# The modulation's matrix-vector product, moved from VectorE and GpSimd to quarters of the TensorE array

## The chip, the cores and the metric

The kernel runs on one core of a Trainium2 chip. A core has TensorE (PE, products), VectorE (DVE), ScalarE (ACT), GpSimd (POOL) and SyncE (SP, which here only issues transfers). The metric is the device time of one execution in microseconds (us). Before the change it is 2470.45 us, the median of three runs (2469.16 to 2474.44).

## The reference

Two blocks of a network for 512 tokens of width 2048, all in float32. The change touches the start of the first block, where a vector `c` of length 2048 gives each channel a shift, a scale and a gate:

```
c_act = silu(c)
mod = c_act @ w_ada + b_ada              # 2048 -> 3 * 2048
shift, scale, gate = split(mod, 3)
h = rms_norm(x) * (1 + scale) + shift
proj = h @ w_in                          # 2048 -> 5184
... recurrent branch, attention branch, their outputs y
x = x + gate * (y @ w_out)
```

The product `c_act @ w_ada` is one row times a matrix of 50 MB: little arithmetic per weight. Its first two thirds (shift and scale) are needed before any product with `w_in`, the last third (gate) only after both branches. A second block and a gated embedding follow.

## The kernel before

The tokens are kept transposed: a tile is 128 channels on the partitions by 512 tokens, and x is 16 such tiles, `xT[0]` to `xT[15]`. A product in float32 precision is made of three products in the faster type fp32r: each operand is split into a high part (a rounded copy, ScalarE) and a low part (the rest, VectorE), names `whi`, `wlo`, `hh`, `hl`, and `mm3` issues three TensorE products. These are the "split products" below. A product on unsplit float32 operands is used in few places: the sums over partitions with a tile of ones (`pnx`, `pada`) and `pR`, which spreads the norm over the partitions.

The program is written out in full, and a planner fixes its order: a "spine" of units (a block of weights, its split, its products) is walked in order, and side work written as generators is put between the products when the estimated clocks of class `Clock` say that what it waits for is there. Each engine then runs its own queue strictly in that order. SP's queue holds the loads; a load waits there until the buffer that it reuses is free, and everything behind it waits too. There are 78 buffers of 2 KB per partition for most tiles and 10 of 4 KB for weights.

The start of the spine is the embedding product (`pple`, 96 split products), meanwhile the squares of x are summed. Then come the products with `w_in`: `pearly` (four output tiles that are summed up in PSUM, two channel tiles at a time), `pp` (the others, in parts), later `ppan`. Those with channel tiles 2g and 2g+1 need group g of the modulation.

The modulation comes in eight groups `ada_group(g)`. A group is 16 pieces `wada` of 128 x 512 weights: piece k holds the rows of `w_ada` that meet `ccol[:, k]`, and its columns are the shifts and scales of 256 channels. VectorE multiplies most pieces by their `ccol` and adds them to one sum (`stt`, line 302); for the others ScalarE multiplies (line 314) and GpSimd adds them to a second sum (line 287). GpSimd joins the two, `ada_sum` adds over the partitions with four products with ones (`pada`), then `modT` gets the bias and `modulate` applies it to two tiles of x and splits them into `hh` and `hl`. Group 0 keeps its two sums apart. The gate (`ada_gate`) does the same with 64 pieces `wgate` in four groups, every second piece by ScalarE and GpSimd, while the recurrent branch (`prg`, `pig`, `xcl`) runs.

Of the kernel before, what the change touches and what calls it, by code (L numbers as in the profile page):

```python
# [11 lines left out]
AF = mybir.ActivationFunctionType  # L12
OP = mybir.AluOpType
# [8 lines left out]
NSLOT, NW = 78, 10                   # buffers of 2 KB and of 4 KB in each partition  # L22
LD, LS = 4, 3                        # units of weights loaded ahead, and split ahead
GSPLIT = (2, 3, 4, 5)                # first units, of which GpSimd takes the low parts
ADALD0, ADALD = 16, 4                # pieces of the modulation's weights loaded ahead, for the first group and later
POOL0, POOL = (1, 3, 4, 6, 8, 10), (1, 4, 7, 10, 13)  # pieces that ScalarE and GpSimd take
XF = 8                               # tiles of x loaded before the rest of the embedding's weights
XK = (2, 5, 6, 8, 10, 12, 14, 15)    # tiles of x squared before each of the first blocks of that product is copied
RB = 12                              # block of that product at which the norm of x starts
PLEG = 4                             # group of the modulation from which the product is stored  # L30
ORDER = (0, 1, 2, 10, 3, 11, 4, 12, 5, 13, 6, 14, 7, 15)  # columns of the first projection: 0-7 gate, 8-15 recurrence
GATEN = 4                            # position in that order at which the modulation's gate starts
FILL = (2, 3, 3, 3, 5)               # tiles of the first output between the pairs of heads
UPB, UPM = 3, 26                     # lead of the up projection of b; tile of the merge gates at which its loads start
WIDTH, STEPS = 2, 2                  # recurrences in flight; steps of one generator at a time
BACKLOG, LATE = 3.0, 5.0             # how far the other engines' work may run ahead of TensorE's (us, estimated)
# [3 lines left out]
def consts():  # L40
    """Constants that depend on shapes alone."""
# [43 lines left out]
def blocks():  # L85
    """The blocks (rows of tiles from, to, (columns from, to), ..) in which the weights are read."""
# [60 lines left out]
class Clock:  # L147
    """Rough times of the engines, by which the work is interleaved; nothing depends on it but the order."""
# [32 lines left out]
class Sides:  # L181
    """Work that is interleaved with the stream of projections: each generator yields the tiles that it waits for."""
# [54 lines left out]
class Unit:  # L237
    def __init__(self, src, shape, mm, pre=None, hold=1, half=False):
        """hold: the units whose weights are done with after this one; half: weights in the small slots."""
        self.src, self.shape, self.mm, self.pre, self.hold, self.half = src, shape, mm, pre, hold, half  # L240
        self.raw = self.hi = self.lo = None


def emit(ctx, tc, I, out):
# [122 lines left out]
    # ---------------------------------------------------------------- constants and loads  # L367
# [25 lines left out]
    # silu of c  # L393
# [13 lines left out]
    # ---------------------------------------------------------------- per-layer embedding product  # L407
# [36 lines left out]
    # ---------------------------------------------------------------- x, its norm, and the modulation  # L444
# [10 lines left out]
    def row_rsqrt(ssum, name, keep_cols=None, flag=None):  # L455
        """1 / rms of each token, on all partitions, from the sums of squares that each partition holds."""
# [25 lines left out]
    def x_stats():  # L482
# [15 lines left out]
        tt(xT[0], xT[0], R_["x"], OP.mult)  # L498
        gtt(xT[1], xT[1], R_["x"], OP.mult)
# [13 lines left out]
    def ada_sum(accs, js):  # L513
        ps = bank("pada")
        for j, jj in enumerate(js):
            for i, a in enumerate(accs):
                mm(ps[:, j:j + 1], a[:, jj * 128:(jj + 1) * 128], ones[:, 0:1], i == 0, i == len(accs) - 1)
        return ps

    def ada_group(g):  # L520
        accs = [slot([128, 512], "aacc") for _ in range(2)]
        a3 = [a.rearrange("p (s n) -> p s n", s=2) for a in accs]
        for k in range(16):
            w = ada_raw.pop((g, k))
            j = k in (POOL if g else POOL0)
            if g and k in (6, 9):
                x = xT[2 * g + k // 9]
                gtt(x, x, R_["x"], OP.mult)
            yield EAGER, [w]
            if k == 0:  # L530
                ts(a3[0], w, ccol[:, 0:1], None, OP.mult)
            elif k == 1:
                act(a3[1], w, AF.Identity, scale=ccol[:, 1:2])
            elif j:
                act(w, w, AF.Identity, scale=ccol[:, k:k + 1])
                gtt(a3[1], a3[1], w, OP.add)
            else:
                stt(a3[0], w, ccol[:, k:k + 1], a3[0], OP.mult, OP.add)
            ada_dma(g * 16 + k + 1 + (ADALD0 if g == 0 else ADALD))
            if g >= PLEG and stores:  # L540
                dma("G", *stores.pop(0))
        yield accs if g else accs[1:]
        r0 = WHERE["b_ada"]
        k0 = 2 * g
        if g == 0:
            ps = ada_sum(accs[1:], range(4))
            pre = small("apre")
            tt(pre[:, 0:2], ps[:, 0:2], cols[:, r0:r0 + 2], OP.add)
            stt(pre[:, 2:4], ps[:, 2:4], 1.0, cols[:, r0 + 16:r0 + 18], OP.add, OP.add)
            while issued["split"] < 6:  # L550
                split_next()
            yield accs[:1]
            ps = [ada_sum(accs[:1], (i, 2 + i)) for i in range(2)]
            while "scaled" not in ada:
                ada["stuck"] = True
                yield
            for i in range(2):
                tt(modT[:, i:i + 1], ps[i][:, 0:1], pre[:, i:i + 1], OP.add)
                tt(modT[:, 16 + i:17 + i], ps[i][:, 1:2], pre[:, 2 + i:3 + i], OP.add)
                modulate(i)  # L560
            dma("Q", cst[:, 128:], I["cst"][:, 128:])
            return
        gtt(accs[0], accs[0], accs[1], OP.add)
        yield accs[:1]
        ps = ada_sum(accs[:1], range(4))
        tt(modT[:, k0:k0 + 2], ps[:, 0:2], cols[:, r0 + k0:r0 + k0 + 2], OP.add)
        stt(modT[:, 16 + k0:18 + k0], ps[:, 2:4], 1.0, cols[:, r0 + 16 + k0:r0 + 18 + k0], OP.add, OP.add)
        for k in (k0, k0 + 1):
            modulate(k)

# [23 lines left out]
    def ada_gate():  # L594
# [11 lines left out]
        load(4)  # L606
        yield

        def sums(c, a):
            ps = ada_sum([a], range(4))  # L610
# [3 lines left out]
        due = None  # L614
        for c in range(4):
# [1587 lines left out]
```

## Time and profile before

| | |
|---|---|
| median of three runs | 2470.45 us |
| the profiled execution, its span | 2470.8 us |
| PE busy | 2389.4 us, 97% |
| VectorE, ScalarE, GpSimd busy | 62%, 39%, 16% |
| mean granted TensorE clock | 0.983 |

The profile is one execution on the chip. The span is cut in 40 slices on its page; digits are tenths of busy time, and `PEclk` the granted clock. All that the change touches lies in the first seven slices, of 62 us each:

```
PE   6898988999999999999999999999999999999998
DVE  7777899558786537747887725777424345333336
PEclk8998989999999999999999999999999999999999
```

A true float32 product shows as two records, each with its own load of weights; a split product as one. Matmuls are pipelined, so the time from one start to the next is what a product costs, not its shown length.

### The profile page before, as it was taken

What the parts mean: (1) busy time and instruction counts of PE and PEld (TensorE: products, weight loads), DVE (VectorE), ACT (ScalarE), POOL (GpSimd) and SP (SyncE); (2) the same over time, 40 slices, a digit from 0 to 9 for tenths busy, and PEclk for the clock granted to TensorE, in tenths of its full rate; (3) what the DMA queues carried; (4) which work ended last, traced back from release to release, by engine and by line L of the source; (5) the groups of instructions that cost most, each with busy time, mean ns of one, the idle gap of its engine ahead of it and who ended that gap; (6) DMA issues with size and microseconds to landing.
All of it is one profiled execution on the core that took longest, in us unless ns stands there. A gap on an engine that the chain in (4) does not pass through costs nothing.

```text
span 2470.8 us, 31047 instructions
## 1 busy us (share of the span) xinstructions
PE 2389.4 (97%) x11491; PEld 2007.0 (81%) x11491; DVE 1524.6 (62%) x2771; ACT 975.8 (39%) x1792; POOL 406.6 (16%) x479
## 2 busy tenths in 40 slices
PE   6898988999999999999999999999999999999998
PEld 5676766988888998888888888888888888888887
DVE  7777899558786537747887725777424345333336
ACT  5533555445443334334444414444323222222223
POOL 3454345023221200100000000000001200111201
PEclk8998989999999999999999999999999999999999
DMA  8775554233235533422222222222335633444633
GB/s 301 249 259 194 186 185 150 86 119 122 101 107 179 165 103 102 129 90 90 95 86 90 90 94 94 93 88 86 113 123 182 229 112 107 134 138 141 221 99 123
DMA packets 114760, 336.98 MB, mean 136 GB/s; under 512 B 15326, under 2 KB 15620, under 8 KB 114608
## 3 DMA queue, kind: packets, MB, share of 16 engines
q1 hardware_dynamic: 89712, 256.63, 31.7%
q0 software_dynamic: 24032, 77.22, 9.2%
q8 instruction: 90, 1.47, 0.2%
q10 hardware_dynamic: 864, 1.14, 0.1%
q14 instruction: 62, 0.51, 0.1%
HBM read 297.18 MB, written 37.75 MB: 136 GB/s over the span
## 4 chain that ended last, share of the span: by engine, by line
PE 71%; issue 10%; DVE 3%; DMA 1%; POOL 1%; ACT 0%; POOLq 0%; SPq 0%; DVEq 0%; ACTq 0%
PE pch L320 43%; PE ppan L320 11%; PE po L320 6%; PE psc L320 3%; PE pO L320 3%; PE pPT L324 2%; DVE wlo L283 1%; DVE agacc L302 0%; DVE cA L283 0%; DMA sguw<-in_sgu_w_dram 0%; PE pcs L320 0%; PE px L324 0%; DMA w1r<-in_cmp_w_k_dram 0%; PE pqT L324 0%; PE pcT L324 0%
## 5 line engine op out<-in xcount | busy, mean ns | idle before, releaser
L283 DVE TENSOR_TENSOR wlo<-wraw,whi 128x1024 fp32r<-128x1024 f32 (+5 forms) x399 | 479.3, 1203 | 219.3 <-ACT whi L314 214.0
L314 ACT ACTIVATE whi<-wraw 128x1024 fp32r<-128x1024 f32 (+5 forms) x403 | 399.8, 1002 | 287.5 <-PE pch L320 107.8
L320 PE MATMUL pch<-h2h,whi 128*128 128x512 f32 x1216 | 483.5, 398 | 0.0
L320 PE MATMUL pch<-h2h,wlo 128*128 128x512 f32 x1216 | 474.5, 390 | 0.0
L320 PE MATMUL pch<-h2l,whi 128*128 128x512 f32 x1216 | 474.4, 390 | 0.0
L320 PEld LDWEIGHTS pch<-h2h,wlo 128*128 128x128 f32 x1216 | 228.3, 188 | 49.2
L320 PEld LDWEIGHTS pch<-h2h,whi 128*128 128x128 f32 x1216 | 228.7, 188 | 41.2
L320 PEld LDWEIGHTS pch<-h2l,whi 128*128 128x128 f32 x1216 | 229.0, 188 | 40.5
L314 ACT ACTIVATE P<-psc,sm 128x512 f32<-128x512 f32 (+3 forms) x160 | 83.8, 527 | 137.1 <-DVE sm L306 101.8
L320 PE MATMUL pp<-hh,wlo 128*128 128x512 f32 x320 | 129.1, 403 | 6.8 <-DVE wlo L283 6.8
L320 PE MATMUL pp<-hh,whi 128*128 128x512 f32 x320 | 130.2, 407 | 2.2 <-DVE acc L283 2.2
L320 PE MATMUL pp<-hl,whi 128*128 128x512 f32 x320 | 129.1, 404 | 0.0
L320 PE MATMUL ppan<-whi,x2h 128*128 128x512 f32 (+1 forms) x320 | 111.0, 347 | 0.0
L320 PE MATMUL ppan<-whi,x2l 128*128 128x512 f32 (+1 forms) x320 | 110.9, 347 | 0.0
L320 PE MATMUL ppan<-wlo,x2h 128*128 128x512 f32 (+1 forms) x320 | 110.9, 347 | 0.0
L320 PE MATMUL pch<-mgh,whi 128*128 128x512 f32 x256 | 101.1, 395 | 0.0
L320 PE MATMUL pch<-mgh,wlo 128*128 128x512 f32 x256 | 99.9, 390 | 0.0
L320 PE MATMUL pch<-mgl,whi 128*128 128x512 f32 x256 | 99.7, 389 | 0.0
L320 PE MATMUL pch<-oh,whi 128*128 128x512 f32 x256 | 99.6, 389 | 0.0
L320 PE MATMUL pch<-ol,whi 128*128 128x512 f32 x256 | 99.6, 389 | 0.0
L320 PE MATMUL pch<-oh,wlo 128*128 128x512 f32 x256 | 99.6, 389 | 0.0
L314 ACT ACTIVATE PTh<-pPT 128x512 fp32r<-128x512 f32 (+1 forms) x120 | 59.6, 527 | 93.2 <-PE pPT L324 90.7
(502 smaller groups left out, 4910.1 us busy)
## 6 DMA issues: line engine op xcount, KB each, us to landing
wraw<-in_w_in_dram SPq DMA_DIRECT2D x199, 512.0 KB, 3.5
wada<-in_w_mod_dram SPq DMA_DIRECT2D x128, 256.0 KB, 5.4
wraw<-in_w_out_dram SPq DMA_DIRECT2D x64, 512.0 KB, 3.5
wgate<-in_w_gate_dram SPq DMA_DIRECT2D x64, 256.0 KB, 4.3
wraw<-in_w_ple_gate_dram SPq DMA_DIRECT2D x28, 512.0 KB, 3.5
sg<-mg POOLq DMA_DIRECT2D x32, 256.0 KB, 2.4
wraw<-in_w_up_b_dram SPq DMA_DIRECT2D x16, 512.0 KB, 3.5
sgl<-sg POOLq DMA_DIRECT2D x32, 256.0 KB, 6.2
```

Source lines behind the costliest of these rows:

```text
L283: V.tensor_tensor(o, a, b, op=op)
L314: A.activation(o, a, fn, **k)
L320: T.matmul(o, l, r, start=start, stop=stop_)
L324: T.transpose(o, a, i)
```

## The change

The raw pieces of weights go to TensorE as the moving operand of true float32 products. Before, `cc` is filled: 16 blocks of 32 columns, the first column of block k is `ccol[:, k]`, the others are zero. Four pieces make a set: piece k0 + q is multiplied with its block of `cc` and lands in partitions 32q to 32q + 31 of one PSUM bank, so the four products of a set use the four column quarters of the array. Four sets sum up in PSUM (`start`, `stop`); the bank is copied, and `pada` adds over its 128 partitions, of which four are not zero. VectorE takes all scalings of x by the norm. Eight pieces are loaded ahead instead of four; in the gate eight, then twelve.

```diff
-ADALD0, ADALD = 16, 4
+ADALD0, ADALD = 16, 8
...
     def x_stats():
...
-        tt(xT[0], xT[0], R_["x"], OP.mult)
-        gtt(xT[1], xT[1], R_["x"], OP.mult)
+        for k in range(2):
+            tt(xT[k], xT[k], R_["x"], OP.mult)
...
+    cc = slot([128, 16, 32], "cc")
+
+    def ada_spread():
+        V.memset(cc, 0.0)
+        vcopy(cc[:, :, 0:1], ccol[:, :, None])
+
+    def ada_quad(acc, ws, k0, nk=16):
+        for q, w in enumerate(ws):
+            T.matmul(acc[32 * q:32 * q + 32, :], cc[:, k0 + q, :], w, start=k0 == 0, stop=k0 == nk - 4)
+        clock.note("PE", 1.2, [acc], ws)
...
     def ada_group(g):
-        accs = [slot([128, 512], "aacc") for _ in range(2)]
-        a3 = [a.rearrange("p (s n) -> p s n", s=2) for a in accs]
-        for k in range(16):
-            w = ada_raw.pop((g, k))
-            j = k in (POOL if g else POOL0)
-            if g and k in (6, 9):
-                x = xT[2 * g + k // 9]
-                gtt(x, x, R_["x"], OP.mult)
-            yield EAGER, [w]
-            if k == 0:
-                ts(a3[0], w, ccol[:, 0:1], None, OP.mult)
-            elif k == 1:
-                act(a3[1], w, AF.Identity, scale=ccol[:, 1:2])
-            elif j:
-                act(w, w, AF.Identity, scale=ccol[:, k:k + 1])
-                gtt(a3[1], a3[1], w, OP.add)
-            else:
-                stt(a3[0], w, ccol[:, k:k + 1], a3[0], OP.mult, OP.add)
-            ada_dma(g * 16 + k + 1 + (ADALD0 if g == 0 else ADALD))
-            if g >= PLEG and stores:
-                dma("G", *stores.pop(0))
+        acc = bank("pmod")
+        for k0 in range(0, 16, 4):
+            ws = [ada_raw.pop((g, k)) for k in range(k0, k0 + 4)]
+            if g and k0 in (4, 8):
+                x = xT[2 * g + k0 // 8]
+                tt(x, x, R_["x"], OP.mult)
+            yield EAGER, ws
+            ada_quad(acc, [w.rearrange("p s n -> p (s n)") for w in ws], k0)
+            ada_dma(g * 16 + k0 + 4 + (ADALD0 if g == 0 else ADALD))
+            for _ in range(4):
+                if g >= PLEG and stores:
+                    dma("G", *stores.pop(0))
+        yield [acc]
+        a = slot([128, 512], "aacc")
+        act(a, acc, AF.Copy)
+        yield [a]
...
-        gtt(accs[0], accs[0], accs[1], OP.add)
-        yield accs[:1]
-        ps = ada_sum(accs[:1], range(4))
+        ps = ada_sum(a, range(4))
+        while "scaled" not in ada:
+            ada["stuck"] = True
+            yield
...
     def ada_gate():
...
-                elif k % 2:
-                    act(w, w, AF.Identity, scale=ccol[:, k:k + 1])
-                    gtt(accs[1], accs[1], w, OP.add)
-                else:
-                    stt(accs[0], w, ccol[:, k:k + 1], accs[0], OP.mult, OP.add)
-                load(i + 5)
...
+                w4 = [ws.pop(i + q) for q in range(4)]
+                yield w4
+                ada_quad(acc, w4, k0)
+                load(i + 12)
+            yield [acc]
+            a = slot([128, 512], "agacc")
+            act(a, acc, AF.Copy)
```

`begin()` calls `ada_spread()` after the first splits. The special handling of group 0 and its `pre` goes; comments go too, so line 320 of before is 319 after. Because the planner's estimates change, the order of the whole start changes.

On PE, from the end of the embedding product (`pple`) to the first product with modulated x (`pearly`), before:

```order
L320 MATMUL pple<-wlo,pTh_213 128x512
L320 MATMUL pple<-whi,pTl_214 128x512
L320 MATMUL pR<-dg,ones 128x128 x4
L320 MATMUL pada<-ones,aacc 128x1 x8
L320 MATMUL pearly<-hh_616,whi 128x512
L320 MATMUL pearly<-hl_617,whi 128x512
```

and after, from the sum of squares (`pnx`) on, where `pmod` is the bank of a group's four sets, 16 products here:

```order
L319 MATMUL pnx<-ones,xacc 128x1 x4
L522 MATMUL pmod<-wada,cc 32x512 x16
L319 MATMUL pada<-ones,aacc 128x1 x4
L319 MATMUL pR<-dg,ones 128x128 x4
L319 MATMUL pple<-whi,pTh_210 128x512
L319 MATMUL pple<-wlo,pTh_210 128x512
```

All of group 0 now stands ahead of the last 18 `pple` products; before, these came right behind `pnx`, and the sums of group 0 after them. From there on sets stand singly or up to four in a row between `pearly` and `pp` products, in 37 places in all, and the 32 sets of the eight groups are done before the 312 `pp` products that before were spread between the groups.

On SP, from the last tiles of x on, before:

```order
L328 DMA wada<-in_w_mod_dram 128x512 x17
L328 DMA wraw<-in_w_in_dram 128x512
L328 DMA wada<-in_w_mod_dram 128x512 x15
L328 DMA cst<-in_cst_dram 128x544
L328 DMA wraw<-in_w_in_dram 128x512 x2
L328 DMA wada<-in_w_mod_dram 128x512 x3
```

and after:

```order
L327 DMA wada<-in_w_mod_dram 128x512 x16
L327 DMA wraw<-in_w_in_dram 128x512
L327 DMA wada<-in_w_mod_dram 128x512 x16
L327 DMA cst<-in_cst_dram 128x544
L327 DMA wraw<-in_w_in_dram 128x512
L327 DMA wada<-in_w_mod_dram 128x512 x8
L327 DMA wraw<-in_w_in_dram 128x512
L327 DMA wada<-in_w_mod_dram 128x512 x16
```

Up to the second group's load the queue is the same; behind it the pieces of the modulation stand closer together, with fewer blocks of `w_in` between them.

## Rows read from the trace of the kernel before

**Rows 1.** The page: span, and busy time of PE and its weight loads.
```profile
span 2470.8 us, 31047 instructions
...
PE 2389.4 (97%) x11491; PEld 2007.0 (81%) x11491; DVE 1524.6 (62%) x2771; ACT 975.8 (39%) x1792; POOL 406.6 (16%) x479
```
**Rows 2.** Windows: stretch, length, busy us of PE PEld DVE ACT POOL, clock, DMA.
```profile
31.70:254.80 223.10, 188.81 (x773) 152.12 (x773) 173.80 (x220) 92.17 (x138) 108.32 (x81) 0.89 0.68 231
254.80:421.60 166.80, 144.19 (x592) 116.38 (x591) 160.28 (x181) 96.14 (x146) 78.77 (x55) 0.92 0.55 183
421.60:2470.80 2049.20, 2034.67 (x10045) 1721.13 (x10043) 1172.32 (x2347) 764.66 (x1470) 214.00 (x337) 1.00 0.37 119
```
**Rows 3.** Timeline of PE (start, us, form): split products at full and half clock.
```profile
254.11 0.39 PE L320 MATMUL pearly<-hh,whi 128*128 128x512 f32 x1
254.33 0.39 PE L320 MATMUL pearly<-hl,whi 128*128 128x512 f32 x1
...
420.78 0.63 PE L320 MATMUL ppan<-wlo,hh 128*128 128x512 f32 x1
421.20 0.63 PE L320 MATMUL ppan<-whi,hl 128*128 128x512 f32 x1
```
**Rows 4.** Timeline of PE: true float32 products of 1 and 128 columns.
```profile
30.81 1.02 PE L320 MATMUL pnx<-ones,xacc 128*128 128x1 f32 x8
31.69 0.48 PE L320 MATMUL pple<-whi,pTh 128*128 128x512 f32 x1
32.01 0.40 PE L320 MATMUL pple<-wlo,pTh 128*128 128x512 f32 x1
...
850.67 1.05 PE L320 MATMUL pR<-dg,ones 128*128 128x128 f32 x8
851.48 0.41 PE L320 MATMUL ppan<-whi,h2h 128*128 128x360 f32 x1
```
**Rows 5.** Waits of PE in 31.7 to 254.8: us, times, longest.
```profile
PE pada L320 <- POOL aacc L287: 17.6, 5, 4.9
PE pR L320 <- DVE dg L292: 6.7, 1, 6.7
PE pp L320 <- DVE wlo L283: 5.0, 2, 3.8
...
PE pearly L320 <- DVE hl L283: 0.5, 1, 0.5
```
**Rows 6.** Waits of PE in 254.8 to 421.6.
```profile
PE prg L320 <- DVE xcl L283: 16.7, 4, 4.4
...
PE ppan L320 <- ACT whi L314: 0.2, 1, 0.2
```
**Rows 7.** Groups in 31.7 to 254.8; above them the tile view's min/median/max.
```profile
L302 DVE SCALAR_TENSOR_TENSOR aacc<-wada,ccol,aacc x79: 737/752/1937, 32.8 to 240.0; 128x512 f32<-128x512 f32 x79
...
L302 DVE SCALAR_TENSOR_TENSOR aacc<-wada,ccol,aacc 128x512 f32<-128x512 f32 x79 | 89.7, 1135 | 1.7
...
L287 POOL TENSOR_TENSOR aacc<-aacc,wada 128x512 f32<-128x512 f32 x33 | 54.6, 1654 | 61.7 <-ACT wada L314 60.8
```
**Rows 8.** Groups in 254.8 to 421.6: the gate; last the tile view.
```profile
L302 DVE SCALAR_TENSOR_TENSOR agacc<-wgate,ccol,agacc 128x512 f32<-128x512 f32 x28 | 31.6, 1128 | 0.2
...
L287 POOL TENSOR_TENSOR agacc<-agacc,wgate 128x512 f32<-128x512 f32 x28 | 45.0, 1606 | 31.4 <-ACT wgate L314 30.3
...
L314 ACT ACTIVATE wgate<-wgate,ccol x28: 704/707/720, 291.7 to 412.3; 128x512 f32<-128x512 f32 x28
```
**Rows 9.** Timeline of ACT: a copy of 128 x 512 from PSUM.
```profile
44.83 0.60 ACT L314 ACTIVATE Rx<-pR 128x512 f32<-128x512 f32 x1 [8.15 <-PE pR L320]
```
**Rows 10.** Timeline of SP's queue: the loads of group 0 and what follows.
```profile
19.66 11.16 SPq L328 DMA_DIRECT2D wada<-in_w_mod_dram  x17
31.26 0.33 SPq L328 DMA_DIRECT2D wraw<-in_w_in_dram  x1
```
**Rows 11.** DMA in 0 to 60 us, 40 slices of 1.5 us.
```profile
GB/s 0 126 350 279 306 391 392 404 412 406 385 388 391 386 391 385 382 391 389 384 385 391 386 384 382 388 388 386 388 392 389 389 376 201 45 0 96 79 0 0
```

More of the change, by code (lines that the diff above doesn't have):

```diff
@@ L24 @@
 GSPLIT = (2, 3, 4, 5)
-ADALD0, ADALD = 16, 4
-POOL0, POOL = (1, 3, 4, 6, 8, 10), (1, 4, 7, 10, 13)
+ADALD0, ADALD = 16, 8
 XF = 8
@@ L511, in ada_dma, with ada_sum @@
             ada_next[0] += 1
-    def ada_sum(accs, js):
+    cc = slot([128, 16, 32], "cc")
[6 more added lines that the diff above has]
+        clock.note("PE", 1.2, [acc], ws)
+    def ada_sum(a, js):
         ps = bank("pada")
         for j, jj in enumerate(js):
-            for i, a in enumerate(accs):
-                mm(ps[:, j:j + 1], a[:, jj * 128:(jj + 1) * 128], ones[:, 0:1], i == 0, i == len(accs) - 1)
+            mm(ps[:, j:j + 1], a[:, jj * 128:(jj + 1) * 128], ones[:, 0:1], True, True)
@@ L542, in ada_group @@
-        yield accs if g else accs[1:]
+        acc = bank("pmod")
[10 more added lines that the diff above has]
+                    dma("G", *stores.pop(0))
@@ L543, in ada_group @@
+        yield [acc]
+        a = slot([128, 512], "aacc")
+        act(a, acc, AF.Copy)
+        yield [a]
         r0 = WHERE["b_ada"]
         k0 = 2 * g
[L545 to L551, printed above, removed]
-            yield accs[:1]
[L553 to L562, printed above, removed]
@@ L563, in ada_group @@
-        gtt(accs[0], accs[0], accs[1], OP.add)
-        yield accs[:1]
-        ps = ada_sum(accs[:1], range(4))
+        ps = ada_sum(a, range(4))
+        while "scaled" not in ada:
+            ada["stuck"] = True
+            yield
         tt(modT[:, k0:k0 + 2], ps[:, 0:2], cols[:, r0 + k0:r0 + k0 + 2], OP.add)
@@ L569, in ada_group @@
             modulate(k)
+        if g == 0:
+            dma("Q", cst[:, 128:], I["cst"][:, 128:])
     def modulate(k):
@@ L604, in load @@
                 nxt[0] += 1
-        load(4)
+        load(8)
         yield
-        def sums(c, a):
-            ps = ada_sum([a], range(4))
+        for c in range(4):
+            acc = bank("pmod")
+            for k0 in range(0, 16, 4):
+                i = 16 * c + k0
+                w4 = [ws.pop(i + q) for q in range(4)]
[5 more added lines that the diff above has]
+            act(a, acc, AF.Copy)
+            yield [a]
+            ps = ada_sum(a, range(4))
             r0 = WHERE["b_ada"] + 32 + 4 * c
             tt(modT[:, 32 + 4 * c:36 + 4 * c], ps[:, 0:4], cols[:, r0:r0 + 4], OP.add)
-        due = None
-        for c in range(4):
-            accs = [slot([128, 512], "agacc") for _ in range(2)]
-            for k in range(16):
-                i = 16 * c + k
-                w = ws.pop(i)
-                yield [w]
-                if k == 0:
-                    ts(accs[0], w, ccol[:, 0:1], None, OP.mult)
-                elif k == 1:
-                    act(accs[1], w, AF.Identity, scale=ccol[:, 1:2])
-                elif k % 2:
-                    act(w, w, AF.Identity, scale=ccol[:, k:k + 1])
-                    gtt(accs[1], accs[1], w, OP.add)
-                else:
-                    stt(accs[0], w, ccol[:, k:k + 1], accs[0], OP.mult, OP.add)
-                load(i + 5)
-                if k == 6 and due:
-                    sums(c - 1, due)
-            gtt(accs[0], accs[0], accs[1], OP.add)
-            due = accs[0]
-        yield [due]
-        yield [due]
-        sums(3, due)
     acc1 = {}
@@ L2150, in begin @@
         ple_prep()
+        ada_spread()
         fetch(2)
```

## The prediction

> **What bounds the kernel now.** I read the page first: TensorE (PE) is busy 2389.4 of 2470.8 us [rows 1]. Read as an average that leaves nothing to win and says that every product added to PE costs its full time. So I cut the span where the change ends. From 31.7 us, where the first sum over tokens is through PE, to 254.8 us, the last `pearly` product, is stage 1 (the first eight groups of the modulation); from there to 421.6 us, where the gate's last sums start, is stage 2; the rest has 2034.7 busy of 2049.2 us and PE at full clock [rows 2]. What can be won lies in the 390 us of the two stages.
>
> There I compared PE's time with what its work takes when nothing waits. Consecutive 512-column products of the split kind start 0.227 us apart at full clock and 0.425 at half [rows 3]. The sums over partitions with `ones` are true float32; four of them show as eight records in 0.88 us, so 0.22 us each, in pairs of 0.11 [rows 4]. Stage 1 holds, by the order of the program, 690 split products, 4 for `pR` and 36 for `pada`: 690 x 0.227 + 40 x 0.22 = 165.4 us. It takes 223.1, so 57.7 are lost. Stage 2 holds 567 and 12: 131.3 of 166.8 us, 35.5 lost. The waits of PE name 34.4 us of the first loss (six rows; `pada` waiting for GpSimd's sum of the two partial sums is half of it) and 22.7 of the second (four rows; `prg` waiting for VectorE is 16.7) [rows 5, 6]. What is left, 23 and 13 us, is the mean granted clock of 0.89 and 0.92 [rows 2], that is time at 1.2 of the two levels (1.2 and 2.4 GHz) after such waits, and restarts.
>
> Why VectorE (DVE) is late is in the groups: in stage 2 it is busy 160.3 of 166.8 us, 31.6 of it the gate's multiply-adds, whose mean of 1.13 us is half as much again as the median of 0.75 that the same form has in stage 1; GpSimd (POOL) works on the same pieces meanwhile, 1.61 us each [rows 2, 7, 8].
>
> **What goes.** From VectorE 79 + 28 multiply-adds (89.7 + 31.6 us) and the twelve that start a sum; from GpSimd 33 + 28 adds (54.6 + 45.0) and the joins; from ScalarE 33 + 28 scalings and 12 starts, some 0.71 us each [rows 7, 8]. VectorE takes over the 15 scalings of x that GpSimd did. None of this is on PE; it counts only by the 93 us that PE loses.
>
> **What comes.** 192 float32 products with 32 output partitions and 512 columns, four to a set, so 48 sets, 32 in stage 1 and 16 in stage 2. A set has four products by the code, and eight pairs by the way float32 shows in rows 4. No row has a float32 product of 512 columns, nor one on a quarter of the array. Bounds for one pair: at best the 0.227 us of a split product with as many columns; at worst four times the 0.11 us of a 128-column pair, 0.44 [rows 3, 4]. The 128-column pairs (0.101 us each, as short as pairs of one column) are bounded by loading weights, so 0.44 is an upper bound, but they are the nearest rows of this kind, and I take 0.44, 0.88 a product. The four quarters: at best all at once, 0.45 to 0.88 a set; at worst one after another, 1.8 to 3.5. I take all at once, plus 0.2 for going into the set and out of it (the product after a block of sums starts its follower 0.32 instead of 0.227 us later, so 0.1 on each side [rows 4]): **1.1 us a set, 48 x 1.1 = 52.8 us**.
>
> The Trainium skill (TensorE: Matmul & The Clock Gate, Part 3: Packing small matmuls) says that products on different strips run at once, and gives 2.38 times for three column strips. Taken as it stands for these sets, 3.5 / 2.38 = 1.5 us would be an estimate, 18 us more over 48 sets and an end near 2468; no run here shows it. Against the change speaks another page of the Trainium skill (TensorEngine Tiling (Array Packing), Key Properties): a change of tiling mode drains the array. The sets stand in 37 places, so 74 changes; rows here show none.
>
> Per group there is also one copy from PSUM (0.6 us on ScalarE, as the copy of `pR` [rows 9]) where the join was, on the chain to x and not on PE; `pada` has 4 products in every group, 4 fewer in all (-0.9 us). Clearing and filling `cc` on VectorE falls before the first split of weights and delays nothing.
>
> **Waits that remain.** PE's queue is in order, and now it holds the sets themselves, so a late piece of weights stops PE. Behind each set stand the `pearly` and `pp` products, and behind those the release of the buffers for which SP's queue waits. Up to the last piece of group 7, SP moves 112 pieces and 6 short blocks of 0.262 MB, 10 long blocks of 0.524, and GpSimd's queue the 16 stores of `pleo`, now together: some 40.7 MB from 31.3 us on [rows 10]. At the 390 GB/s that the slices of the first 45 us show [rows 11] that is 104 us, so the last lands near 139 us with 3 to 5 us of landing. PE reaches the last set of stage 1 near 140 us without waits. They are level, so I allow 12 us of waits and half clock: 1 for the copy before the first `pada`, 5 where two groups follow with little PE work between, 6 for the half clock behind those. Zero and the 57.7 of now are the ends. After the last set some 400 products run with no modulation between them. In stage 2 VectorE has 160 - 36 = 124 us of work or less in 150, so `prg` waits shrink but don't vanish: 8 us for 35.5.
>
> **Sum.** Stage 1: 165.4 - 0.9 + 32 x 1.1 + 12 = 211.7 for 223.1, -11.4. Stage 2, to the end of the same four sums: 131.3 + 0.9 + 16 x 1.1 + 8 = 157.8 for 167.9, -10.1. Together -21 us: 2449.5 from the profiled 2470.8 us, which stands 0.4 us from the median of 2470.45. I say **2450 us**. The break-even is a set of 1.1 + 21.5 / 48 = 1.55 us with these waits; longer sets hide some of them (the weights are then early), which puts it near 1.7.
>
> **Rivals.**
> *The queue keeps the quarters half apart (slower).* The two pairs of one product use the same quarter, so the second waits for the first. If PE starts strictly in the order of its queue, the next quarter's first pair starts only beside that second pair: a set is then five steps of 0.44 us, four when another set follows directly: 48 x 4 x 0.44 + 37 x 0.44 = 100.8 us, 2.1 a set, 48 more than I took. PE is then the bound everywhere and the waits fall to 4 and 3: stage 1 164.5 + 67 + 4 = 235.5 (+12), stage 2 132.2 + 33.6 + 3 = 169 (+1): 2484 us. It decides from 1.7 us a set. For it: records of one product stand in that order [rows 4]; against: no row shows whether a pair on another quarter may pass. The Trainium skill (TensorE: Matmul & The Clock Gate, Part 3) says that products start and end in strict order; by that rule this rival holds, if a pair takes 0.44.
> *No overlap at all.* 48 x 3.5 = 169 us: stage 1 164.5 + 113 + 2, stage 2 132.2 + 56 + 2, +79: 2550 us. Against it: the output quarters are disjoint.
> *The weights set the pace (slower).* If buffers come free late, as now, where SP moves 231 GB/s over stage 1 [rows 2], 40.7 MB take 176 us, the last set stands near 207 and stage 1 ends 97 later, +49: 2510 us with stage 2's gain. It decides below 323 GB/s, where the last set falls behind 157 us. Against it: most pieces reuse a buffer that a set read a group earlier.
> *A pair takes 0.227.* All at once a set is 0.65: 21.6 us less, of which stage 1's waits for weights take back a few: 2431 us.
> *It gains but the waits stay.* With 25 instead of 12 us in stage 1 and 16 in stage 2 the sum is 2470: no change.
>
> **How the numbers follow.** Forecast 0.50, short pairs 0.05, waits stay 0.09, half apart 0.27, weights 0.05, no overlap 0.04. A measurement of this kernel tells 0.2%, 5 us, from none. Faster: 0.48 of the forecast's cases and the short pairs, 0.53; same: 0.02 of the forecast, 0.07 of "waits stay" and 0.03 of "half apart", 0.12; slower: the rest, 0.35. The forecast's own range is 2436 to 2464 (sets of 0.9 to 1.3 us, waits of 12 to 28). The range of 8 in 10 reaches from 2434 to 2490, over the half-apart case.
>
> **What would show it.** Sets: the spacing from the first `pmod` record of a set to the product behind it, 1.1 us (2.1: half apart; 3.5: none). Starts inside a set: eight records within 0.5 us of two instants, or a staircase of 0.44. Place of the last `pearly`: 243 us, the last gate sums near 400. `pada` no longer waits for GpSimd; PE's waits in stage 1 name `wada` transfers. VectorE in stage 2 below 85%. I am wrong if a set takes over 1.7 us, or if PE waits over 30 us for `wada` or `wgate`.

## The result, and the profile after

The changed kernel takes 2459.27 us (median of four runs, 2458.75 to 2459.55), the kernel before 2471.35 us (2469.16 to 2474.44) beside it. The ratio is 0.9948, with a 95% interval of 0.9934 to 0.9962: 12 us faster. The forecast was 2450, 21 us faster; the direction holds and 2459 lies in the range, but the gain is little more than half, and it does not lie where the forecast put it.

The page after, which answers to [rows 1]:

```profile
span 2457.0 us, 31387 instructions
...
PE 2421.9 (99%) x11867; PEld 1994.9 (81%) x11867; DVE 1379.3 (56%) x2665; ACT 938.8 (38%) x1730; POOL 258.7 (11%) x392
```

PE is busy for 32 us more in a span that is 14 us shorter. Whether that is good or bad the page can't say. The windows can (stretch, length, busy us of PE, PEld, DVE, ACT, POOL, clock, DMA share, GB/s; they answer to [rows 2], with bounds moved to the same places of the program):

```profile
29.70:255.30 225.60, 214.27 (x1019) 146.90 (x1020) 80.45 (x145) 74.11 (x107) 16.55 (x26) 0.96 0.65 231
255.30:410.00 154.70, 153.63 (x734) 112.05 (x733) 117.32 (x165) 87.05 (x128) 27.75 (x25) 1.00 0.57 198
```

Stage 1 takes 225.6 us for 223.1 before: the 11.4 us that the forecast took off are not there, although VectorE has less than half of its former work in it (80 for 174 us) and GpSimd almost none. In stage 2 PE runs almost without a break (153.6 of 154.7 us), at full clock. To compare stages without choosing window bounds I use three marks: the first `pnx`, the last `pearly<-hh,whi`, and the first `pcT`, a transpose behind the recurrent branch. After (tile views: duration min/median/max in ns, first and last start):

```profile
L319 PE MATMUL pnx<-ones,xacc x8: 242/250/250, 28.8 to 29.6; 128*128 128x1 f32 x8
L319 PE MATMUL pearly<-hh,whi x64: 389/389/793, 50.2 to 254.7; 128*128 128x512 f32 x64
L323 PE MATMUL pcT<-cst,cq x16: 272/272/273, 454.0 to 459.9; 128*128 128x128 f32 x16
```

From the same rows of every kernel below (us; "stage 1" is from `pnx` to the last `pearly`, "stage 2" from there to `pcT`; the median against the kernel before that ran beside it):

| kernel | `pnx` | first `pearly` | stage 1 | stage 2 | median, and against before |
|---|---|---|---|---|---|
| before | 30.8 | 49.5 | 223.3 | 213.8 | 2471.35 |
| changed | 28.8 | 50.2 | 225.9 | 199.3 | 2459.27, -12.1 |
| gate_only | 28.1 | 47.0 | 222.4 | 199.4 | 2456.71, -15.4 |
| groups_only | 28.7 | 46.7 | 227.2 | 215.7 | 2475.38, +3.2 |
| set_twice | 29.7 | 48.6 | 243.3 | 212.0 | 2488.46, +16.3 |
| one_quarter | 28.4 | 54.2 | 300.0 | 240.1 | 2572.28, +100.1 |
| split_first | 28.7 | 46.4 | 223.0 | 199.3 | 2455.45, -15.7 |
| start_order | 30.0 | 46.0 | 214.8 | 199.3 | 2448.08, -23.1 |
| start_split | 28.9 | 43.0 | 212.9 | 199.2 | 2445.86, -25.3 |
| start_fill | 29.3 | 43.4 | 209.0 | 199.3 | 2443.15, -28.8 |
| dve_back | 28.6 | 46.9 | 227.4 | 205.5 | 2465.84, -5.5 |
| pool_back | 28.8 | 46.5 | 226.8 | 223.2 | 2484.00, +12.7 |
| both_back | 28.4 | 47.0 | 227.3 | 231.5 | 2490.79, +19.5 |
| pool_apart | 28.3 | 46.4 | 226.8 | 213.7 | 2474.17, +2.2 |

The change in one line: stage 1 +2.6, stage 2 -14.5, the rest unchanged (2002.9 us from `pcT` to the end of the span before, 2003.0 after). `pnx` lies between 28.1 and 30.8 us from kernel to kernel, so its 2 us are not put down to the change.

The price of a set, the step that I was least sure of, is right. Timeline of PE after (start, us, form); the first two rows are from an answer that ends at 92.0 us, in the middle of a set:

```profile
91.29 0.39 PE L319 MATMUL pp<-hh,wlo 128*128 128x512 f32 x1
91.61 0.64 PE L522 MATMUL pmod<-wada,cc 128*32 128x512 f32 x4
...
91.61 1.06 PE L522 MATMUL pmod<-wada,cc 128*32 128x512 f32 x8
92.61 0.50 PE L319 MATMUL pp<-hh,whi 128*128 128x512 f32 x1
...
56.11 1.92 PE L522 MATMUL pmod<-wada,cc 128*32 128x512 f32 x16
57.96 0.50 PE L319 MATMUL pearly<-hh,whi 128*128 128x512 f32 x1
58.30 0.40 PE L319 MATMUL pearly<-hl,whi 128*128 128x512 f32 x1
```

A set lasts from 91.61 to 92.61, and 0.09 us more pass before it than between two split products (0.32 for 0.23); as much passes behind the product that follows it (0.34 for 0.23, last two rows): 1.2 us. Of its eight records, four have started by 92.0 us and the other four follow: the first halves of all four products run together, and then the second halves. Two sets in a row take 1.85 us, so a further set costs 0.85. For 48 sets in 37 places that is 37 x 1.2 + 11 x 0.85 = 53.8 us, 1.1 a set.

Now the waits. PE after, in stage 1 and (last row, an answer for 255.3 to 420 us) in stage 2, for the 34.4 and 22.7 us of [rows 5, 6]:

```profile
PE pearly L319 <- ACT whi L313: 8.6, 2, 4.6
PE pmod L522 <- DMA wada<-in_w_mod_dram: 1.4, 3, 0.7
PE pada L319 <- ACT aacc L313: 0.7, 1, 0.7
PE pearly L319 <- POOL wlo L286: 0.6, 1, 0.6
...
PE prg L319 <- DVE xcl L282: 1.1, 2, 0.8
```

The waits for GpSimd's sums are gone, as forecast. The transfers, which I feared, are named for 1.4 us; that is not all that they cost. Where the pieces of a set are still landing, TensorE takes one product after the other as its piece comes and counts as busy in between, as in the three sets (24 records) at 71 us:

```profile
71.01 2.37 PE L522 MATMUL pmod<-wada,cc 128*32 128x512 f32 x12
73.81 1.67 PE L522 MATMUL pmod<-wada,cc 128*32 128x512 f32 x4 [0.43 <-DMA wada<-in_w_mod_dram]
75.80 3.08 PE L522 MATMUL pmod<-wada,cc 128*32 128x512 f32 x8 [0.32 <-DMA wada<-in_w_mod_dram]
78.81 0.50 PE L319 MATMUL pp<-hh,whi 128*128 128x512 f32 x1
```

They take 7.8 us at full clock, where three sets in a row cost 3 x 0.85 + 0.15 = 2.7; the named waits are 0.75 of the 5.1 us. The tile view of `wada` for 60 to 80 us has the rest at the load of `cc` into the array ahead of each product (PEld): eight waits for a piece, 5.5 us. By the same sum the four sets of group 0 lose 2.2 us beyond the waits named there, and the set at 79.70 us 0.8. So transfers cost some 8.8 us in stage 1: 1.4 named, 7.4 inside sets.

The largest named waits are two for `whi`, high parts of weights that ScalarE makes. Timeline of PE at both:

```profile
50.18 0.50 PE L319 MATMUL pearly<-hh,whi 128*128 128x512 f32 x1 [3.93 <-ACT whi L313]
...
105.66 0.79 PE L319 MATMUL pearly<-hh,whi 128*128 128x512 f32 x1 [4.62 <-ACT whi L313]
```

and of ScalarE:

```profile
42.74 0.60 ACT L313 ACTIVATE pleo<-pple 128x512 f32<-128x512 f32 x1 [5.44 <-PE pple L319]
43.23 0.59 ACT L313 ACTIVATE Rx<-pR 128x512 f32<-128x512 f32 x1
...
48.98 0.63 ACT L313 ACTIVATE hh<-xT 128x512 fp32r<-128x512 f32 x1
49.51 1.65 ACT L313 ACTIVATE whi<-wraw 128x512 fp32r<-128x512 f32 x3
...
101.33 0.81 ACT L313 ACTIVATE xT<-xT,modT 128x512 f32<-128x512 f32 x1 [1.93 <-DVE modT L301]
...
104.56 2.94 ACT L313 ACTIVATE whi<-wraw 128x1024 fp32r<-128x1024 f32 x3
```

ScalarE is busy for a third of stage 1 and still late, by the order of its queue. At 42.74 it has stood 5.4 us at a copy of the embedding product that TensorE has not finished, and the copy of the norm, `Rx`, is behind it, though `pR` was issued before that product. At 49.5 and 104.6 the split of the weights stands behind the whole `modulate` of two tiles (`xT`, `hh`, twice), and ahead of the second of these ScalarE idles 1.93 us for `modT`. For group 0 the kernel before had a loop that split the weights ahead of `modulate`; the change took it out with the special handling of that group:

```diff
-            while issued["split"] < 6:
-                split_next()
```

The mean granted clock is 0.79 of full speed in 29.7 to 45.9 us, 0.88 up to 60, and 0.83 in 100 to 120 (windows of the same trace, below with the runs that mend it). In windows of 1 us it is at half from 37.4 to 44.3 us, after the last products of group 0, which TensorE took one by one with two waits of 0.7 us; from 51.1 to 54.5 us, just after the first wait for `whi`; and from 102.3 to 109.1 us, from within the second.

So the theory was: *stage 1 loses its gain to the order of queues, ScalarE's and TensorE's own at the start; stage 2 gains because the other engines are free of the gate's product.* The rival for stage 1: the transfers, at 387 to 396 GB/s until 100 us, set the pace and would take back whatever a better order gives.

### The profile page after: what moved, and what is told of

Read it like the earlier page. It is cut to its first block, busy times and chain, and to the rows that moved or that the text cites. A ratio compares the mean times of both kernels' runs of the same rounds, so it can differ in the third digit from the quotient of the medians.

```text
span 2457.0 us, 31387 instructions
## 1 busy us (share of the span) xinstructions
PE 2421.9 (99%) x11867; PEld 1994.9 (81%) x11867; DVE 1379.3 (56%) x2665; ACT 938.8 (38%) x1730; POOL 258.7 (11%) x392
## 4 chain that ended last, share of the span: by engine, by line
PE 84%; issue 10%; DVE 2%; DMA 2%; POOL 1%; ACT 1%; SPq 0%; POOLq 0%; DVEq 0%; ACTq 0%
PE pch L319 43%; PE ppan L319 14%; PE pp L319 8%; PE po L319 5%; PE psc L319 3%; PE pO L319 3%; PE pearly L319 2%; PE pPT L323 2%; PE pmod L522 2%; PE pple L319 1%; DVE wlo L282 0%; DMA wada<-in_w_mod_dram 0%; DVE cA L282 0%; DMA sgub<-in_sgu_b_dram 0%; PE pada L319 0%
## 5 line engine op out<-in xcount | busy, mean ns | idle before, releaser
L282 DVE TENSOR_TENSOR wlo<-wraw,whi 128x1024 fp32r<-128x1024 f32 (+5 forms) x399 | 464.7, 1167 | 249.0 <-ACT whi L313 243.5
```

What stands on the lines that cost most here:

```text
L282: V.tensor_tensor(o, a, b, op=op)
```

## Experiments: one part alone

**gate_only** is the kernel before with the new `ada_gate`, `ada_quad` and `cc`; **groups_only** the changed kernel with the `ada_gate` of before.

> Only the gate runs as sets of four products on TensorE; the eight groups of shift and scale stay on VectorE, ScalarE and GpSimd as before. Theory (the gain of the change is stage 2's, 14 us by the landmarks of the two traces, and stage 1 gave back what it won): 2457 us, 2454 to 2461, with the first `pcT` about 14 us earlier than before and the last `pearly` at about 255 us. Rival (both stages gained what was forecast, and stage 1 only looks unchanged because its end is marked badly): about 10 us, 2461 or more. Rival (stage 2 gains only when the start is changed too, since the order of the whole start moves): 2466 to 2471.

> Only the eight groups run as sets on TensorE; the gate stays on VectorE, ScalarE and GpSimd as before. Theory: stage 1 loses in new waits what it wins, so 2470 us, 2467 to 2474, no change. Rival (stage 1 gained its forecast 11 us): 2459 to 2461.

Measured: 2456.71 us, ratio 0.9937 (0.9924 to 0.9949), and 2475.38 us, 1.0014 (1.0005 to 1.0022). By the table the gate gives 14.4 us in stage 2 and hardly anything else; the groups alone make the kernel 3 us slower, and the two add up to the change (-15.4 + 3.2 = -12.2). The first came out as the theory said; the second 1.4 us above its range. Two thirds of the sets, 32 of 48, bought nothing in this order.

## Experiments: the price of a set

**set_twice** issues each set twice (with half of `ccol` in `cc`; not shown):

```diff
-            T.matmul(acc[32 * q:32 * q + 32, :], cc[:, k0 + q, :], w, start=k0 == 0, stop=k0 == nk - 4)
+            T.matmul(acc[32 * q:32 * q + 32, :], cc[:, k0 + q, :], w, start=k0 == 0, stop=False)
+        for q, w in enumerate(ws):
+            T.matmul(acc[32 * q:32 * q + 32, :], cc[:, k0 + q, :], w, start=False, stop=k0 == nk - 4)
```

> Every set of four products is issued twice into the same sum, with half the multiplier, so the result is the same and TensorE has 48 sets more to do. By the trace of the changed kernel a further set in a row takes 0.84 us. Theory (TensorE is the bound of stage 2 and of the last third of stage 1, and the waits of the first two thirds of stage 1 hide about half of the added sets there): 16 x 0.84 + 32 x 0.84 less 6 to 10 us, so +32 us, 2491 (2485 to 2500). Rival (stage 1 is paced by the transfers of weights, so sets there are hidden wholly): +16, 2475. Rival (a set costs more than its starts show, 1.07 us each time): +51, 2510.

**one_quarter** writes all four products to the same quarter (the copy and `pada` then read its 32 partitions; not shown):

```diff
-            T.matmul(acc[32 * q:32 * q + 32, :], cc[:, k0 + q, :], w, start=k0 == 0, stop=k0 == nk - 4)
+            T.matmul(acc[0:32, :], cc[:, k0 + q, :], w, start=k0 + q == 0, stop=k0 + q == nk - 1)
```

> The four products of a set all write the same 32 partitions of the bank, so they can't stand beside each other; the sum over partitions then reads 32 partitions. Theory (the four quarters run at once, and a product alone is two halves of 0.42 to 0.44 us): a set takes 3.4 to 3.5 us, 48 x 2.4 = 115 us more, less 10 to 25 us of stage 1's waits that it hides: 2559 us (2545 to 2578). Rival (a half takes 0.227 us when it does not share the array): 1.8 us a set, +36: 2490 to 2500. Rival (the quarters save nothing): 2460.

Measured 2488.46 and 2572.28 us, both in the range of the theory. Timeline of PE in set_twice:

```profile
334.75 1.06 PE L522 MATMUL pmod<-wgate,cc 128*32 128x512 f32 x8
335.63 1.04 PE L524 MATMUL pmod<-wgate,cc 128*32 128x512 f32 x8
336.60 0.50 PE L319 MATMUL pp<-hh,whi 128*128 128x512 f32 x1
```

and in one_quarter:

```profile
366.53 3.62 PE L522 MATMUL pmod<-wgate,cc 128*32 128x512 f32 x8
370.08 0.50 PE L319 MATMUL pp<-hh,whi 128*128 128x512 f32 x1
```

The second set costs 0.88 us; a set without the quarters 3.55, eight halves of 0.44. In stage 2 nearly all of it shows: 12.7 us for 16 further sets (0.79 each), 40.8 for 16 sets of one quarter (2.55 each). In stage 1 some 11 of 28 us of doubled sets are hidden (17.4 shown, for 32 x 0.88), and 6 of 80 of the long ones (74 shown, for 32 x 2.5). So a set costs what was forecast, and the rival by which the transfers pace stage 1, and hide doubled sets wholly, does not hold for the stage as a whole.

## Experiments: the order of the queues in stage 1

**split_first** splits the weights of the next unit ahead of `modulate`:

```diff
         ps = ada_sum(a, range(4))
+        while issued["split"] < (6 if g == 0 else issued["i"] + 1):
+            fetch(issued["split"] + 1)
+            split_next()
         while "scaled" not in ada:
```

> As the changed kernel, but ScalarE and the engine of the low part split the weights of the next `pearly` unit before they modulate x, instead of behind it. Theory (stage 1 lost its gain to the order of ScalarE's queue: the two longest waits of TensorE, 4.3 and 4.9 us, are `pearly` waiting for `whi`, which was queued behind `modulate`): of 4.3 + 4.9 about 5 us go, and 2 us of half clock behind them: 2452 us (2449 to 2455). Rival (until 96 us the transfers set the pace, so what the first wait gives back is lost again where the sets of groups 2 and 3 wait for `wada`): only the second wait counts, 2456 to 2457. Rival (what TensorE waits for is x itself, not its weights): 2459, no change.

**start_order** leaves the sets of group 0 to the planner:

```diff
                     for _ in range(13):
                         sides.advance(ada["x"])
-                        sides.advance(ada["gen"])
```

> As the changed kernel, but the sets of group 0 are not put in a row ahead of the last three blocks of the embedding product: the norm of x goes on alone there, and the sets come where the planner puts them, between and behind those blocks, so TensorE has work while the last pieces of weights land, and the copy of the norm (`Rx`) is no longer behind a copy that waits for TensorE. Theory (queue order cost stage 1 its gain): the first `pearly` comes 5 to 8 us earlier and the end 4 to 6: 2454 us (2451 to 2457). Rival (transfers set the pace until 96 us): the first `pearly` is earlier, but `pmod` waits longer for `wada` in groups 2 and 3, and the end moves by 0 to 2: 2457 to 2460.

**start_split** has both edits:

> Both edits: the sets of group 0 where the planner puts them, and weights split ahead of `modulate`. Theory (queue order): 10 to 12 us of stage 1's 28 us of waits and half clock go: 2448 us (2444 to 2452). Rival (transfers set the pace until 96 us): no better than splitting first alone, 2455 to 2457, with the waits moved to `wada`.

Measured: 2455.45 us (0.9935, 0.9919 to 0.9952), 2448.08 (0.9905, 0.9891 to 0.9920) and 2445.86 (0.9897, 0.9882 to 0.9912). The second and third clearly beat the changed kernel's 0.9948; the first one's interval overlaps with it. The rival, that transfers take the gain back, falls as a whole, but not without a rest: from 55 to 82 us, all at full clock, the sets last 5.9 us longer than their price in the changed kernel, 7.4 in split_first, 4.2 in start_order and 4.7 in start_split, since their pieces are still landing. So 1.5 us of what split_first won were lost there. split_first gave 3.6 us of the 7 expected: its first `pearly` is 3.7 us earlier, and two new waits came, 2.6 and 2.0 us (`pp` for `whi`, `pearly` for `hh`). start_order gave 11.0 against 5: 5.4 us are there at the first `pearly` (from `pnx`), the other 5.7 behind it, since with other clocks the planner also put a later long split ahead of its `modulate`, and the second wait of 4.6 us is gone too. How much of that second part was luck of the planner can't be told from this run. split_first and start_order fell outside their ranges, on opposite sides (2449 to 2455 and 2451 to 2457); start_split lies in its own.

The windows of the changed kernel:

```profile
29.70:45.90 16.20, 14.83 (x67) 9.13 (x67) 4.27 (x20) 2.77 (x5) 0.00 (x0) 0.79 1.05 387
45.90:60.00 14.10, 9.54 (x52) 3.87 (x50) 4.44 (x5) 5.42 (x9) 7.86 (x11) 0.88 1.05 394
60.00:100.00 40.00, 39.26 (x200) 20.64 (x200) 11.72 (x23) 18.99 (x31) 3.78 (x7) 1.00 1.04 396
100.00:120.00 20.00, 15.34 (x70) 9.78 (x69) 7.45 (x10) 7.76 (x10) 0.00 (x0) 0.83 0.68 238
```

and of start_split, the last row its whole stage 1:

```profile
29.80:45.00 15.20, 12.33 (x74) 6.51 (x78) 5.73 (x23) 7.21 (x12) 4.34 (x6) 0.98 1.06 387
45.00:60.00 15.00, 14.91 (x76) 6.41 (x68) 5.26 (x11) 3.90 (x6) 6.84 (x13) 0.91 1.04 407
60.00:100.00 40.00, 38.67 (x196) 23.15 (x200) 13.13 (x20) 20.40 (x31) 0.00 (x0) 1.00 1.05 394
100.00:120.00 20.00, 20.00 (x101) 14.14 (x98) 4.34 (x7) 8.04 (x12) 0.00 (x0) 1.00 0.80 296
...
29.80:242.50 212.70, 208.41 (x1020) 141.66 (x1021) 78.72 (x145) 74.07 (x106) 16.08 (x26) 0.99 0.69 245
```

The transfers run as fast in both up to 100 us; TensorE does more work beside them (74 + 76 records for 67 + 52 in the first 30 us) and stays at full clock at 100 to 120. With the order mended stage 1 takes 212.7 us, with the last `pearly` at 242. The prediction said 211.7 and 243.

**start_fill** has both edits and puts the first two sets of group 1 behind group 0's `pada` (`ada_group` then starts group 1 at its third set; not shown):

```diff
         ps = ada_sum(a, range(4))
+        if g == 0:
+            first[1] = bank("pmod")
+            for n in (0, 4):
+                ws = [ada_raw.pop((1, k)) for k in range(n, n + 4)]
+                ada_quad(first[1], [w.rearrange("p s n -> p (s n)") for w in ws], n)
+                ada_dma(16 + n + 4 + ADALD)
```

> As the kernel with both edits of the start, and the first two sets of group 1 are put right behind group 0's `pada`, where TensorE now stands for 2.1 us and then runs four sets at half clock (0.83 us between halves). Theory (queue order: the wait is filled by 1.9 us of work whose weights landed already, and without the pause less runs at half clock): 2 to 4 us less, 2442 to 2444. Rival (the sets wait for `wada` there instead, or the transfers of group 2 take it back): 2445 to 2447.

Measured 2443.15 us, 0.9882 (0.9866 to 0.9899): 16.1 us less than the changed kernel took, and the fastest that was run. PE's named waits in its stage 1 add up to 2.5 us, 1.2 of them for weights that were still landing (2.6 us more are lost inside the sets between 55 and 82 us):

```profile
PE pmod L521 <- DMA wada<-in_w_mod_dram: 1.2, 2, 0.7
```

## Experiments: which engine's freedom stage 2 gained from

Beside each set of the gate, **dve_back** gives VectorE its two multiply-adds back, **pool_back** ScalarE and GpSimd their scalings and adds, **both_back** both, into sums that nothing reads (in short):

```diff
                 ada_quad(acc, w4, k0)
+                for q in (0, 2):                      # dve_back; the first of a group is a ts
+                    stt(sv[0], w4[q], ccol[:, k0 + q:k0 + q + 1], sv[0], OP.mult, OP.add)
+                for q in (1, 3):                      # pool_back; the first of a group is one act
+                    act(w4[q], w4[q], AF.Identity, scale=ccol[:, k0 + q:k0 + q + 1])
+                    gtt(sv[1], sv[1], w4[q], OP.add)
```

> As the changed kernel, and beside each set of the gate VectorE multiplies and adds two of its four pieces into a sum that nobody reads, as it did before the change (4 + 28 instructions, 25 us at 0.75). Theory A (stage 2 gained 14 us because GpSimd no longer works beside VectorE: every form of VectorE was some 40% longer there, 1.20 for 0.69 us at `xcl`, 1.05 for 0.75 at `xc`): VectorE's own 25 us fit into the 50 us that it now has free, so 0 to +3 us, 2459 to 2462. Theory B (it gained them because VectorE's own share of the products went): +8 to +14, 2467 to 2473.

> As the changed kernel, and beside each set of the gate ScalarE scales the other two pieces and GpSimd adds them into a sum that nobody reads, as before the change (32 and 28 instructions). Theory A (GpSimd beside VectorE stretches it): VectorE's other work of stage 2 takes some 40 us longer while GpSimd adds, TensorE waits for `xcl` again, +4 to +10: 2463 to 2469, with `xcl` over 1 us. Theory B (VectorE's own products): VectorE still has room, 0 to +2, 2459 to 2461.

> Both of these, so that VectorE, ScalarE and GpSimd do in stage 2 what they did before the change, in addition to the sets on TensorE. Theory A and B alike: the 14 us of stage 2 are lost and, since TensorE's sets stand in its waits in part, up to 10 us on top: 2473 to 2484. Rival (stage 2 gained by the order of the program or the loads, not by freed engines): 2459 to 2463.

Measured 2465.84 (6.6 us over the changed kernel), 2484.00 (+24.7) and 2490.79 (+31.5). Neither theory had the sizes: VectorE's own work costs more than A said and less than B, and the other part more than either. The rival of both_back, that the loads or the order gave stage 2 its gain, falls: the gate's weights are loaded as far ahead in these runs as in the changed kernel. For pool_back a row of ScalarE's waits in 255 to 420 us shows why:

```profile
ACT wgate L313 <- PE pmod L522: 15.9, 7, 4.1
```

ScalarE scales each piece in place, and must now wait until TensorE has read it. That is a wait which the kernel before did not have, so **pool_apart** scales into a tile of its own, ahead of the set:

```diff
+                        t = slot([128, 512], "agt")
+                        act(t, w4[q], AF.Identity, scale=ccol[:, k0 + q:k0 + q + 1])
+                        gtt(sv, sv, t, OP.add)
                 ada_quad(acc, w4, k0)
```

> As the run with ScalarE's and GpSimd's part of the gate back, but ScalarE scales into a tile of its own and ahead of the set, so that it no longer waits for TensorE to have read the piece (15.9 us of ScalarE's waits there), and the copy of the gate's sum is not held up by that. Theory C (of the 25 us of that run a part came from this new wait, the rest from GpSimd stretching VectorE's forms): 2465 to 2474, `xc` still over 0.9 us where GpSimd works, `pada` waiting for `agacc` under 4 us. Rival (the wait made no difference): 2480 to 2485. Rival (it made all of it): 2459 to 2461.

Measured 2474.17 us (1.0009, 1.0000 to 1.0019), 14.9 over the changed kernel, 0.2 above the range that was expected; `pada` waits 3.0 us for `agacc`. So about 10 us of pool_back were the new wait. ScalarE's and GpSimd's part by itself takes all of stage 2's gain (213.7 us for 213.8 before), though now with 16 us of sets on TensorE; VectorE's part takes 6. Why can be read from VectorE's instructions in stage 2: min/median/max in ns by the tile view, 255 to 420 us, and for `acc` the group (busy us, mean ns | idle before). Before:

```profile
L302 DVE SCALAR_TENSOR_TENSOR xc<-acc,cols,xc x17: 734/751/1665, 292.8 to 419.9; 128x511 f32<-128x511 f32 x6, 128x510 f32<-128x510 f32 x6, 128x509 f32<-128x509 f32 x5
L283 DVE TENSOR_TENSOR xcl<-xc,xch x7: 675/682/2146, 265.8 to 417.0; 128x512 fp32r<-128x512 f32 x7
...
L283 DVE TENSOR_TENSOR acc<-pp,acc 128x512 f32<-128x512 f32 x20 | 13.6, 679 | 0.0
```

dve_back, where GpSimd is out and VectorE has its share:

```profile
L301 DVE SCALAR_TENSOR_TENSOR xc<-acc,cols,xc x18: 743/750/753, 294.3 to 413.5; 128x511 f32<-128x511 f32 x6, 128x510 f32<-128x510 f32 x6, 128x509 f32<-128x509 f32 x6
L282 DVE TENSOR_TENSOR xcl<-xc,xch x7: 682/686/691, 267.6 to 398.5; 128x512 fp32r<-128x512 f32 x7
```

pool_apart, where GpSimd has its adds and VectorE nothing of the gate:

```profile
L301 DVE SCALAR_TENSOR_TENSOR xc<-acc,cols,xc x17: 745/751/1654, 293.4 to 419.7; 128x511 f32<-128x511 f32 x6, 128x510 f32<-128x510 f32 x6, 128x509 f32<-128x509 f32 x5
L282 DVE TENSOR_TENSOR xcl<-xc,xch x7: 682/686/1753, 266.8 to 405.3; 128x512 fp32r<-128x512 f32 x7
...
L282 DVE TENSOR_TENSOR acc<-pp,acc 128x512 f32<-128x512 f32 x20 | 13.6, 682 | 8.0 <-PE pp L319 8.0
```

Most instructions last as long in all three: 0.75 us (`xc`) and 0.68 (`xcl`). Where GpSimd adds, those that meet an add last up to 1.65 and 2.15 us; without its adds none does. The means of 1.05 and 1.20 us that the expectations name are mixtures of the two. One meeting can be followed from TensorE back to GpSimd in pool_apart:

```profile
326.89 0.50 PE L319 MATMUL prg<-xch,bdw 128*128 128x512 f32 x1 [3.21 <-ACT xch L313]
...
326.21 0.63 ACT L313 ACTIVATE xch<-xc 128x512 fp32r<-128x512 f32 x1 [6.17 <-DVE xc L301]
...
322.02 4.10 DVE L301 SCALAR_TENSOR_TENSOR xc<-acc,cols,xc 128x511 f32<-128x511 f32 x3
...
318.28 6.51 POOL L286 TENSOR_TENSOR again<-again,agt 128x512 f32<-128x512 f32 x4 [3.31 <-ACT agt L313]
```

Three `xc` take 4.10 us for 2.25, and TensorE waits 3.21 us at the end of that chain. TensorE's waits in this stage are 9.3 us for 1.1 in the changed kernel: 6.3 at `prg`, for `xch` and `xcl`, and 3.0 at `pada`; some 10 us at half clock behind them cost up to 5 more. How the rest of the 14.9 us divides between this stretch and the 32 scalings on ScalarE's queue, the runs don't separate.

dve_back's 6.6 us with short `xc` are nearly one wait: `pada` waits 2.8 us for `agacc` up to 309.4 us, and behind it the granted clock is 0.68 up to 320, some 6.8 us at half clock, which costs up to 3.4. ScalarE makes that copy behind an activation (`la`) that had stood 7.5 us for a transfer of `ga`. The changed kernel has no such wait; why it comes here stays open.

## Why the prediction was right in sign and short in size

- *The set* (1.1 us; four quarters at once, 0.44 for a pair, 0.1 on each side): right. 1.0 us plus 0.1 on each side for a lone set, 0.85 to 0.88 for a further one, 1.1 on average, 3.55 on one quarter. The upper bound from [rows 4] was the price: a float32 product of 512 columns is two halves of 0.44.
- *Half apart* (2.1 us a set), *no overlap* (3.5) and *short pairs* fall by the same rows. The Trainium skill (TensorE: Matmul & The Clock Gate, Part 3) says that products start in strict order. As the rival read that, a product's second half holds back the next quarter's first. The trace differs from that reading: the four first halves started before any second. The 2.38 times that the Trainium skill gives in the same part is for three strips; four here give 3.55 / 1.00 = 3.6 times for a lone set.
- *Stage 1's 12 us of waits and half clock* is the step that failed. Measured: 225.6 - (165.4 - 0.9 + 32 x 1.1) = 25.9 us, the figure of the rival "gains but the waits stay". Of the three terms, the copy before `pada` was allowed 1 us and took 0.7; weights still landing were allowed 5 and took some 8.8; half clock was allowed 6. By the granted clock in the three slow windows, between its two levels, some 17 us passed at 1.2 GHz (2 x (1 - 0.79) x 16.2 and so on), 3.8 of them inside waits; the rest costs half its length, 6.7. The largest part has no term at all: 9.2 us in which `pearly` waited for `whi` and `wlo` of weights that had landed. Together that is 25.4 of the 25.9 us. These weights stood in ScalarE's queue, behind `modulate` and behind a copy that waited for TensorE. The sum put that queue at nothing, although the rows were there: the order of PE ahead of the prediction shows group 0's sets, `pada` and `pR` in front of the last 18 `pple` products, each `pple` block has a copy on ScalarE, and the diff takes out group 0's early split. I read that order for PE alone.
- *The weights set the pace* was given 0.05 and falls: its 49 us more didn't come, and the same transfers carried a stage 13 us shorter. But weights that were still landing cost more than the named 1.4 us: 8.8 in the changed kernel, and still 3.8 to 4.7 between 55 and 82 us in the two fastest.
- *Stage 2's 8 us of waits*: too many. 1.1 us named, full clock throughout, and the gate's last sums at 354 us, not near 400. The gain is 14.5 for 10.1. I counted only VectorE's 36 us of gate work as freed; that its other instructions get shorter once GpSimd stops I did not carry into the sum, though my own text set 1.13 us beside 0.75 [rows 7, 8]. That reading compared a mean with a median: in both stages the mean is 1.13 us and the median 0.74 to 0.75, so the form was lengthened in stage 1 as much as in stage 2.
- *The rest unchanged*: right, within 0.1 us. (In the sum, 2470.8 - 21.5 is 2449.3, not 2449.5; it changes nothing.)

The forecast's stage 1 was what this work takes when the queues let it; the kernel that was measured did not let it, and stage 2 made up a part by another 4 us. That 2459 is not further from 2450 is luck to that extent: stage 1 alone missed by 14 us.

## What to carry to other kernels

When work moves from one engine to another, walk the queues of the engines that keep their work: an instruction whose input is ready is late if one ahead of it in its queue waits for something else, and a low busy share hides that. When a side engine is relieved, price its neighbours' instructions anew, not only the ones that vanish. And try the parts alone: here one half of the change gave all of the gain, until the order around the other half was mended.

## What the runs showed of the hardware

- A true float32 product with 32 output partitions and 512 columns costs two halves of 0.44 us; four in separate column quarters cost the same together, first halves and then second halves (0.85 us in a row, 3.55 when they share a quarter).
- TensorE counts as busy while it takes the four products of a set one by one as their weights land: three sets took 7.8 us for 2.7, with 0.75 us named as waits.
- A VectorE instruction that reads two tiles of SBUF and meets one of GpSimd's adds (128 x 512, 1.55 to 1.6 us each) gets longer by up to an add: `xc` from 0.75 to 1.65 us, `xcl` from 0.68 to 1.75 and 2.15; the others keep their time. `acc<-pp,acc`, which reads one tile of PSUM and one of SBUF, stays at 0.68 us in all kernels, also beside the adds. A form with one tile is hit too: `xc<-acc,cols` lasts 0.54 us, and up to 1.51 where GpSimd adds. The Trainium skill (SBUF — State Buffer, SBUF: two separate sides) says that VectorE with two SBUF inputs and a reading GpSimd exclude each other on a shared pair of ports; for the forms with two tiles these rows agree.
